# A whole network in one kernel: another order for router, branch, early tiles and the embeddings' product, and other figures for the planner

## The chip, the core and the metric

The kernel runs on one core of a Trainium2 chip. The time is the device time of one execution in microseconds (us). The core has a tensor engine (PE, with a separate weight load, PEld), a vector engine (DVE), a scalar engine (ACT), GpSimd (POOL), and SyncE (SP), whose queue here issues nearly all transfers. Each engine runs its instructions in the order in which they were written, and waits on semaphores for the others.

## What is computed

One block of three parts, then four layers, all in float32 for 256 tokens of width 1024:

```python
h = rms_norm(x, attn_norm_w);  x = x + hybrid_mixer(h, ...)          # SSD and attention
h = rms_norm(x, moe_norm_w);   x = x + hier_moe(h, ...)              # 4 groups x 8 experts
gate = sigmoid(rms_norm(x, ple_norm_w) @ w_ple_gate)
x = rms_norm(x + gate * (p @ w_ple), final_norm_w)                   # embeddings p: 256 x 256
for i in range(4):                          # short conv, neighborhood attention, hyena, short conv
    x = x + mixer_i(rmsnorm(x, norm_mix_g[i]))
    x = x + swiglu(rmsnorm(x, norm_ffn_g[i]), f_w13[i], f_w2[i])
```

In hier_moe a router chooses for each token the best of 4 groups and in it the best 2 of 8 experts:

```python
gl = h @ w_rg + b_rg;  g_oh = one_hot(top1(gl));  g_w = sum(softmax(gl) * g_oh)
el_sel = einsum("blge,blg->ble", el, g_oh);  top_v, top_i = top_k(el_sel, 2)
comb = g_oh * (one_hot(top_i) * softmax(top_v) * g_w)
out = sum over g, e of (silu(h @ w_gate[g, e]) * (h @ w_up[g, e]) * comb[g, e]) @ w_down[g, e]
```

## The kernel before

Tokens lie along the free axis: x is four tiles of 128 x 2 x 256 (x[0] to x[3]). A dense product is made from high and low halves of its operands, three PE instructions of 256 columns each (high by high, high by low, low by high). Its weights come in half tiles of 512 KB (128 x 1024), called raw, in the order of the list `self.order`. ACT copies the high half (wh), DVE subtracts for the low half (wl). There are 7 raw buffers and 5 pairs of wh and wl (`NRAW`, `NSPLIT`).

The experts' weights are 192 such half tiles, used unsplit. A few are loaded ahead of the routing: some into raw buffers, some into the wh and wl buffers (`load_as`), and `NEARLY` of them (early tiles, transfers named raws) into general slots that are not refilled. A buffer of the first two kinds is refilled by `used_up` once its products are issued.

The experts run in eight rounds r, each of four experts: `gate_up(r, 0)`, then `turn(r-1)` and `down(r-1)` (product yo), `gate_up(r, 1)` and `gated(r)`. `moe_back(r)` splits yo into yoh and yol, multiplies with pT (product yb) and adds to x. The routing gives each expert 32 places; a branch (`past()`, L1594) leads to spare code if an expert has more. In this kernel it stands behind round 0. `later()` computes the places of the next three quarters and stands behind it.

The router is in three functions. `route_evac(j)` takes the last sum of x[j], adds it and scales it (xg); `route_pair(j)` multiplies xg for the scores (lg), sums the squares into a column of the same lg, transposes xg (ht) and splits it into hth and htl. `moe()` takes the root rtm of the sums, scales the scores (r_lg) and then walks through some twenty small DVE steps to the choice r_sel; cnt counts places, ph is the selection matrix, and the products hg gather the tokens of the experts from hth and htl.

The tail: `dense(self.each(px), ...)` computes p @ w_ple from the split px with 48 PE instructions, then `ple()` the gate's product from hx (x scaled and split), whose norm comes late: `late_rms` sums squares (ssq), takes a root on ACT (rb), and the evacuation multiplies by it; then a sigmoid on ACT (pg), a product on POOL or DVE, the sum into x, and the next hx.

What sets the order is a planner in the program that builds the kernel. `Clock.cost` gives each instruction a time. Side work (routing, filters of the hyena, attention heads, `moe_back`) is in generators; `pump` puts their next step into PE's stream when the planner's clock says that its inputs are there. `busy(n)` writes products of ones (warm) that keep PE at work while it waits. So other figures in `cost` change places all over the kernel. All instructions have the line L400 of the helper that issues them; they are told apart by names.

Of the kernel before, what the change touches and what calls it, by code (L numbers as in the profile page):

```python
# [21 lines left out]
D = 1024  # L22
# [259 lines left out]
class Clock:  # L282
# [17 lines left out]
    def cost(self, eng, op, out, ins, args, kw):  # L300
        n = self.size(out)
        if "dma" in op:
            return n * out.shape[0] * 4 / 360e3
        if eng == "tensor":
            if op == "transpose":
                return 2 * n / 2400
            x = args[2]
            if x.dtype == F32R:
                return max(n, 256) / 2400 + 0.002
            side = 4 if args[1].shape[-1] == 32 else 1  # L310
            return max(n * (4 if x.dtype == F32 else 1) / side, 64) / 2400 + 0.002
        if eng == "scalar":
# [101 lines left out]
class Net:  # L414
    def __init__(self, ctx, tc, a, taps=None):
# [26 lines left out]
        for r in range(1, 8):  # L442
            self.order += four(r, 0) + four(r - 1, 2) + four(r, 1)
        self.order += four(7, 2) + whole(range(m + 96, nch))
        self.moe_base = m
# [80 lines left out]
    def early(self):  # L526


        while self.nload < self.moe_tiles[0]:
            yield  # L530
        for n in self.early_tiles:
            c, half = self.order[n]
            t = [self.new("raws", shape=(128, 512)) for _ in range(2)]
            self.raw[n], self.kind[n] = t, "slots"
            for i in range(2):
                o = half * 1024 + i * 512
                self.nc.sync.dma_start(t[i], self.a["wst"][c][:, o:o + 512])
            t0 = self.now()
            while self.now() < t0 + EGAP:
                yield  # L540
# [467 lines left out]
    def hybrid(self):  # L1008
# [166 lines left out]
        self.route_begin()  # L1175
        self.side(self.early())
        self.dense(self.each(mx), 8, 4, self.route_evac)
# [241 lines left out]
    def route_evac(self, j, ps):  # L1419

        nc, v = self.nc, self.v
        self.residual(ps, j)
# [10 lines left out]
    def route_pair(self, j, xg, sq):  # L1433
# [15 lines left out]
        h, l = self.new("hth", F32R), self.new("htl", F32R)  # L1449
        yield from self.split_steps(ps, h, l)  # L1450
        self.htok[j] = (h, l)

    def moe(self):
# [12 lines left out]
        self.wait(lambda: htok[3] is not None)  # L1466
        rt = self.sm("rtm", [128, 2, 1])
        self.root(rt, lg_ps[:, :, 36:37], D)
        V.reciprocal(rt, rt)
        rt = rt[:, :, 0]  # L1470
        self.busy(12)

# [98 lines left out]
        self.tap("comb", comb)  # L1571
        next(filt)
        self.sides.append(self.filt)
        rslot, cslot, c4 = m("rslot", 8, 1), m("cslot", 8), m("c4", 8, 4)
        pT = [None] * 4

        def weights(q):
# [9 lines left out]
            V.tensor_reduce(cslot[:, rs], c4[:, rs, :], axis=AX.X, op=ALU.add)  # L1587
            V.tensor_tensor(cslot[:, rs], cslot[:, rs], rslot[:, rs, 0], op=ALU.mult)

        def past():  # L1590
# [74 lines left out]

        px = [None] * 2

        def embeddings():
            pt = self.ld("pt", shape=(128, 2, 256))
            nc.sync.dma_start(pt, self.a["pT"])  # L1670
            yield
            px[:] = yield from self.split_both(pt, "px")

        for r in range(8):
            if r == 7:
                self.side(embeddings())
# [21 lines left out]
        self.hx, self.ssum = [None] * 8, None  # L1698
        self.pp = [None] * 4

        def ple_evac(j, ps):
            self.pp[j] = self.new("pp")
            S.activation(self.pp[j], ps, AF.Copy)

        self.dense(self.each(px), 2, 4, ple_evac)
        self.wait(lambda: self.hx[0] is not None)

    def moe_back(self, r, yo, pT):
# [9 lines left out]
        for j in range(4):  # L1718
# [77 lines left out]
    def ple(self):  # L1796
# [7 lines left out]
        self.fsum = None  # L1804
        norm = self.side(self.late_rms())

# [310 lines left out]
    def filters(self):  # L2117
# [57 lines left out]
        def order(n, cb):  # L2175
            cs = slice(256 * cb, 256 * cb + 256)
            rows = slice(64 * n, 64 * n + 64)
            if n == 0 and cb:
                yield from fetch(cb)
# [6 lines left out]
            F, SD, hl = [], [], []  # L2186
            pss = []
            for t in range(2):
                first = cb == 0 and n == 0
                ps = self.mm_tile("fl") if first else self.sd("fl")  # L2190
# [4 lines left out]
                pss.append(ps)  # L2195
                if first and t == 0:
                    continue
                if first:
                    yield
                for t2, ps in enumerate(pss) if first else ((t, ps),):  # L2200
                    f = self.new("F")
                    V.tensor_tensor(f, ps, dec[t2], op=ALU.mult)
                    F.append(f)
                yield
# [51 lines left out]

        yield from fetch(0)
        load(1)
        while not self.routing:
            yield  # L2260
        first = order(0, 0)
        for _ in range(3):
            next(first)
            yield
# [205 lines left out]
```

## Time and profile before

| | us |
| --- | --- |
| median of 3 runs | 1831.96 (1830.24 to 1832.25) |
| profiled execution, its own time | 1834.63 |
| its span in the profile | 1832.8 |
| PE busy | 1764.5 (96%) |
| DVE busy | 1252.2 (68%) |
| ACT busy | 1019.1 (56%) |
| POOL busy | 514.1 (28%) |
| mean granted clock of PE | 0.986 of full speed |

The span is the time from the first to the last instruction in the trace. Busy time says which engine was at work, not which one was waited for; a wait is read from what stood idle and what ended it. The network goes through in this order: the hybrid mixer to 317 us, router and experts to 563, the gate with the embeddings to 606, then the four layers.

### The profile page before, as it was taken

The numbers are of one execution on the slowest core, as the hardware profiler recorded it, in microseconds if no ns is written. First come the engines' busy times: TensorE is split into PE (matmuls) and PEld (weight loads), VectorE is DVE, ScalarE is ACT, GpSimd is POOL, SyncE is SP. The second block draws the span as 40 slices with busy tenths as digits, with TensorE's granted clock in tenths as the row PEclk, the third lists the DMA queues.
The fourth block names the chain that finished last, engine by engine and source line by source line (L and its number), as shares of the span: only waits on it lengthen the run. The fifth ranks groups of instructions, "written<-read, shape, count | busy, mean of one in ns | idle before, by whom it ended". The sixth has DMA issues, their size and how long they took to land. (4 is left out here: it accounts for less than half of the span.)

```text
span 1832.8 us, 30301 instructions
## 1 busy us (share of the span) xinstructions
PE 1764.5 (96%) x11603; PEld 1491.7 (81%) x11603; DVE 1252.2 (68%) x1758; ACT 1019.1 (56%) x1754; POOL 514.1 (28%) x532
## 2 busy tenths in 40 slices
PE   9999999888888899999999999999899999999998
PEld 8897899453236899888987888899898888888887
DVE  6677655322125987886687788668978876888873
ACT  7787644332225656554566655566556555666552
POOL 3635440242440341220122122017611210501210
PEclk9999999998999999999999999999999999999999
DMA  8443359799998575555544455565435555656552
GB/s 284 145 147 116 116 171 337 274 402 406 409 406 292 166 246 180 188 187 181 184 150 147 146 185 186 174 206 174 150 118 193 189 181 182 190 163 210 184 191 74
DMA packets 114909, 377.14 MB, mean 206 GB/s; under 512 B 12449, under 2 KB 22057, under 8 KB 114761
## 3 DMA queue, kind: packets, MB, share of 16 engines
q1 hardware_dynamic: 114568, 375.03, 60.1%
q8 instruction: 92, 1.51, 0.3%
q14 instruction: 57, 0.46, 0.1%
q0 software_dynamic: 48, 0.13, 0.0%
q10 hardware_dynamic: 144, 0.00, 0.0%
HBM read 369.87 MB, written 5.25 MB: 205 GB/s over the span
## 5 line engine op out<-in xcount | busy, mean ns | idle before, releaser
L400 PE MATMUL mm<-hx,wh 128*128 128x256 f32 (+1 forms) x3712 | 936.1, 331 | 7.3 <-ACT hx L400 5.1
L400 DVE TENSOR_TENSOR wl<-raw,wh 128x1024 fp32r<-128x1024 f32 (+1 forms) x486 | 681.2, 1411 | 214.9 <-ACT wh L400 192.5
L400 PE MATMUL mm<-hx,wl 128*128 128x256 f32 x2576 | 727.6, 282 | 0.6 <-DVE wl L400 0.6
L400 PEld LDWEIGHTS mm<-hx,wh 128*128 128x128 f32 x3712 | 628.4, 191 | 86.8 <-issue 8.5
L400 ACT ACTIVATE wh<-raw 128x1024 fp32r<-128x1024 f32 (+1 forms) x486 | 507.9, 1053 | 294.6 <-PE mm L400 133.6
L400 PEld LDWEIGHTS mm<-hx,wl 128*128 128x128 f32 x2576 | 491.0, 191 | 1.2 <-DVE wl L400 1.2
L400 PE MATMUL mm<-fx,wh 128*128 128x512 f32 x704 | 248.9, 399 | 0.0
L400 POOL TENSOR_TENSOR t<-mo,rb 128x512 f32<-128x512 f32 x80 | 103.5, 1293 | 406.1 <-DVE mo L400 393.0
L400 PE MATMUL mm<-fx,wl 128*128 128x256 f32 x704 | 197.7, 281 | 0.0
L400 PEld LDWEIGHTS mm<-fx,wh 128*128 128x128 f32 x704 | 132.3, 188 | 33.0
L400 PEld LDWEIGHTS mm<-fx,wl 128*128 128x128 f32 x704 | 133.0, 189 | 0.0
L400 POOL TENSOR_TENSOR acc<-acc,sq 128x512 f32<-128x512 f32 x20 | 33.5, 1677 | 315.9 <-ACT sq L400 315.8
L400 DVE TENSOR_TENSOR mo<-mo,mm 128x256 f32<-128x256 f32 x220 | 82.5, 416 | 21.3 <-ACT mo L400 21.3
L400 ACT ACTIVATE fx<-t 128x256 fp32r<-128x256 f32 x88 | 36.5, 416 | 104.6 <-DVE t L400 104.6
L400 ACT ACTIVATE mo<-mm 128x256 f32<-128x256 f32 x220 | 73.7, 375 | 35.9 <-PE mm L400 35.1
L400 PE MATMUL gu<-raw,hg 128*32 128x512 f32 x468 | 78.7, 624 | 3.7 <-DMA raw<-in_wst 3.7
L400 PE MATMUL mm<-yx,wh 128*128 128x256 f32 (+1 forms) x320 | 69.8, 308 | 0.0
L400 DVE TENSOR_TENSOR fx<-t,fx 128x256 fp32r<-128x256 f32 x88 | 37.3, 425 | 37.7 <-ACT fx L400 37.7
L400 ACT ACTIVATE hx<-x,vec 128x256 fp32r<-128x256 f32 x72 | 32.8, 502 | 53.1 <-DVE x L400 51.2
L400 PEld LDWEIGHTS mm<-yx,wh 128*128 128x128 f32 x320 | 51.8, 191 | 4.3 <-issue 1.3
L400 PE MATMUL mm<-yx,wl 128*128 128x256 f32 x192 | 54.2, 282 | 0.0
L400 PEld LDWEIGHTS gu<-raw,hg 128*32 128x32 f32 x468 | 15.9, 112 | 45.6 <-DMA raw<-in_wst 22.0
(389 smaller groups left out, 2443.3 us busy)
## 6 DMA issues: line engine op xcount, KB each, us to landing
raw<-in_wst SPq DMA_DIRECT2D x663, 512.0 KB, 4.7
raws<-in_wst SPq DMA_DIRECT2D x22, 256.0 KB, 7.4
hs<-H SPq DMA_DIRECT2D x16, 256.0 KB, 5.2
Hl<-hs SPq DMA_DIRECT2D x16, 256.0 KB, 11.3
tb<-in_rpbt SPq DMA_DIRECT2D x16, 192.0 KB, 4.8
dec<-in_decay SPq DMA_DIRECT2D x8, 256.0 KB, 7.1
x<-in_xT SPq DMA_DIRECT2D x4, 256.0 KB, 5.1
raw<-in_wst SPq DMA_DIRECT2D x4, 256.0 KB
```

The costliest lines, as they stand in the source:

```text
L400: return f(*args, **kw)
```

## The change

It rewrites five places.

1. The planner's figures: a product costs 0.0135 us beside its columns where it cost 0.002, and a transfer goes at 400 GB/s where it went at 360. The distance between filter steps (FGAP) is 18 instead of 20, the number of early tiles (NEARLY) 13 instead of 11, and their distance (EGAP) 1.3 instead of 1.5. The early tiles begin behind those in raw, wh and wl buffers, and `moe()` issues the rest of them at its start.
2. The router: for the last tile, x is added in halves, the root is taken ahead of the transposes, and htl is made by ACT (htf) and POOL instead of DVE. One DVE step of the choice is gone. The first filter's products, which stood ahead of lg, come later.
3. The branch stands behind round 1, `later()` ahead of `gate_up(1, 1)`.
4. The embeddings' product is side work from round 6 on, with its own transfers (wp, four of 256 KB), splits (wph, wpl) and products (pp, four groups of 12).
5. The gate: the table of the root is loaded in `moe_back` of round 7, that of the sigmoid right after the root; two of four products are on DVE.

```diff
-NRAW, NSPLIT, NSLOT, NLOAD, WARM, LAG, FGAP, BMOST, PARK = 7, 5, 46, 6, 11, 4.0, 20, 12, 14
-NEARLY, EGAP = 11, 1.5
+NRAW, NSPLIT, NSLOT, NLOAD, WARM, LAG, FGAP, BMOST, PARK = 7, 5, 46, 6, 11, 4.0, 18, 12, 14
+NEARLY, EGAP = 13, 1.3
...
-            return n * out.shape[0] * 4 / 360e3
+            return n * out.shape[0] * 4 / 400e3
...
-                return max(n, 256) / 2400 + 0.002
+                return max(n, 256) / 2400 + 0.0135
...
-        self.early_tiles = range(2 * m + NRAW, 2 * m + NRAW + NEARLY)
+        first = 2 * m + NRAW + 2 * NSPLIT
+        self.early_tiles = range(first, first + NEARLY)
...
-            t0 = self.now()
-            while self.now() < t0 + EGAP:
+            t0, self.clock.mark = self.now(), 0.0
+            while self.now() < t0 + EGAP and not self.routing:
...
+        if j < 3:
+            self.residual(ps, j)
         for o in range(2):
+            if j == 3:
+                nc.vector.tensor_tensor(self.x[j][:, o, :], self.x[j][:, o, :], ps[:, o, :], op=ALU.add)
             nc.scalar.activation(xg[:, o, :], self.x[j][:, o, :], AF.Copy, scale=v("moe", 2 * j + o))
...
+        if j == 3:
+            self.rtok = self.sm("rtm", [128, 2, 1])
+            self.root(self.rtok, self.lg_ps[:, :, 36:37], D)
+            nc.vector.reciprocal(self.rtok, self.rtok)
         ps = self.sd("ht", reads=2)
...
-        yield from self.split_steps(ps, h, l)
+        if j == 3:
+            f = self.new("htf")
+            nc.scalar.activation(h, ps, AF.Copy)
+            nc.scalar.activation(f, ps, AF.Copy)
+            nc.gpsimd.tensor_tensor(l, f, h.bitcast(F32), op=ALU.subtract)
+        else:
+            yield from self.split_steps(ps, h, l)
...
-        filt = self.filt[0]
-        next(filt)
-        next(filt)
+        self.busy(6)
+        while self.ahead in self.sides:
+            self.step(self.ahead)
...
-        tt(oh2, oh2, bc(tm8), op=ALU.is_equal)
-        tt(oh2, oh2, bc(goh), op=ALU.mult)
+        tt(oh2, rev8, bc(tm8), op=ALU.is_equal)
...
+            for j in range(4):
+                w = self.new("wp", shape=(128, 512))
+                nc.sync.dma_start(w, self.a["wst"][self.moe_base + 96][:, 512 * j:512 * j + 512])
...
+                for k in range(2):
+                    for o in range(2):
+                        i = slice(128 * (2 * k + o), 128 * (2 * k + o) + 128)
+                        self.three(ps[:, o, :], h[:, i], l[:, i], px[k], k == 0 and o == 0, k == 1)
...
         for r in range(8):
-            if r == 7:
+            if r == 6:
                 self.side(embeddings())
...
+            if r == 1:
+                self.side(later())
             gate_up(r, 1, ps)
+            self.wait(lambda: r // 2 in weighed)
             gated(r, ps)
-            if r == 0:
+            if r == 1:
                 past()
-                self.side(later())
                 self.routed = True
...
-        self.dense(self.each(px), 2, 4, ple_evac)
...
+                if j == 0:
+                    nc.scalar.activation(self.sm("warm4", [128, 1]), self.eps, AF.Sqrt)
...
+        def scale():
+            yield from self.late_rms()
+            S.activation(self.sm("warm5", [128, 1]), self.eps, AF.Sigmoid)
...
-            eng = V if j == 3 else G
+            eng = V if j in (0, 3) else G
...
-        yield from self.flow([first] + [order(n, cb) for cb in range(4) for n in range(2)][1:], FGAP, 2)
+        yield from self.flow([order(n, cb) for cb in range(4) for n in range(2)], FGAP, 3)
```

SP's queue from the last early tiles to the branch, before (raws are early tiles, raw those in buffers, `mosti` the number that the branch looks at):

```order
L400 DMA raw<-in_wst 128x1024
L400 DMA raws<-in_wst 128x512 x2
L400 DMA raw<-in_wst 128x1024 x11
L400 DMA raws<-in_wst 128x512 x2
L400 DMA raw<-in_wst 128x1024 x7
L1592 TENSOR_LOAD mosti
L1592 ISA x2
L1594 COMPARE_AND_BRANCH
```

The same place of the changed kernel:

```order
L400 DMA raw<-in_wst 128x1024
L400 DMA raws<-in_wst 128x512 x4
L400 DMA raw<-in_wst 128x1024 x39
L1602 TENSOR_LOAD mosti
L1602 ISA x2
L1604 COMPARE_AND_BRANCH
```

Before, the last two halves of an early tile stood behind eleven other tiles, and seven tiles stood between them and the branch; now all early tiles stand ahead, and 39 tiles stand between them and the branch.

ACT in the tail, from the splits ahead of the root rb to the sigmoids pg, before:

```order
L400 ACTIVATE sq<-x_98 128x512
L400 ACTIVATE wh<-raw 128x1024 x2
L400 ACT_TABLE_LOAD
L400 ACTIVATE rb<-ssq,eps 128x256
L400 ACTIVATE wh<-raw 128x1024 x2
L400 ACT_TABLE_LOAD
L400 ACTIVATE pg<-pg 128x512 x3
```

The same place of the changed kernel:

```order
L400 ACTIVATE sq<-x_98 128x512
L400 ACTIVATE pp<-pp 128x512
L400 ACTIVATE wh<-raw 128x1024
L400 ACTIVATE rb<-ssq,eps 128x256
L400 ACT_TABLE_LOAD
L400 ACTIVATE warm_6340<-eps 128x1
L400 ACTIVATE wh<-raw 128x1024 x2
L400 ACTIVATE pg<-pg 128x512 x3
```

The load ahead of rb has gone to an earlier place, and the one ahead of pg stands right behind rb, ahead of two splits.

PE in the neighborhood attention, between the first head's sums qkn and its transposes qkt, as a difference:

```order
 L400 MATMUL mm<-hx,wh 128x256 x2
 L400 MATMUL mm<-hx,wl 128x256
-L400 MATMUL mm<-hx,wh 128x256 x2
-L400 MATMUL mm<-hx,wl 128x256
-L400 MATMUL mm<-hx,wh 128x256 x2
-L400 MATMUL mm<-hx,wl 128x256
-L400 MATMUL mm<-hx,wh 128x256 x2
-L400 MATMUL mm<-hx,wl 128x256
 L400 MATMUL qkt<-cst,sqq 128x128 x2
```

Nine products of the dense stream that stood ahead of qkt stand behind it now; for the four groups of heads the distances were 18, 19, 34 and 32 products and are 9, 6, 23 and 28.

## Rows read from the trace of the kernel before

**Rows 1.** busy by stretch: us; PE, PEld, DVE, ACT, POOL; clock; DMA share; GB/s
```profile
0.00:317.00 317.00, 308.45 (x2333) 281.58 (x2334) 206.56 (x343) 213.79 (x377) 131.85 (x141) 0.99 0.56 185
317.00:563.30 246.30, 211.85 (x1352) 99.81 (x1350) 60.53 (x140) 62.61 (x128) 88.43 (x104) 0.94 0.97 380
563.30:606.50 43.20, 35.28 (x259) 34.23 (x259) 33.03 (x38) 29.34 (x41) 8.04 (x5) 0.92 0.71 241
606.50:1832.80 1226.30, 1208.95 (x7662) 1076.06 (x7662) 952.06 (x1239) 713.38 (x1209) 285.81 (x283) 1.00 0.54 175
```

**Rows 2.** the same view, the experts' stretch at and behind the branch
```profile
345.00:357.00 12.00, 12.00 (x90) 4.88 (x83) 0.00 (x0) 2.69 (x5) 1.48 (x2) 0.90 0.70 234
357.00:561.00 204.00, 175.94 (x1082) 78.82 (x1080) 48.95 (x90) 52.20 (x109) 80.64 (x96) 0.95 1.03 406
```

**Rows 3.** timeline of SP's queue: start, us until the last issue, engine, line, transfer
```profile
318.29 1.56 SPq L400 DMA_DIRECT2D raws<-in_wst  x2
333.97 18.14 SPq L400 DMA_DIRECT2D raw<-in_wst  x13
```

**Rows 4.** waits of SP, and instructions of the branch, 327 to 352
```profile
SPq L1594 <- SPq L1594: 8.5, 4, 5.0
...
L1594 PEldq COMPARE_BRANCH  x1: 6252/6252/6252, 338.1 to 338.1; - x1
```

**Rows 5.** timelines of PE, ACT and DVE in the router
```profile
320.17 1.09 PE L400 MATMUL ht<-cst,xg 128*128 128x128 f32 x4
...
321.79 0.26 ACT L400 ACTIVATE rtm<-lg,eps 128x2 f32<-128x2 f32 x1
...
321.93 0.69 DVE L400 TENSOR_TENSOR htl<-ht,hth 128x512 fp32r<-128x512 f32 x1 [3.74 <-ACT hth L400]
322.53 0.16 DVE L400 RECIPROCAL rtm<-rtm 128x2 f32<-128x2 f32 x1
322.72 0.42 DVE L400 SCALAR_TENSOR_TENSOR r_lg<-lg,rtm,vec 128x36 f32<-128x36 f32 x2
...
326.15 0.22 DVE L400 TENSOR_TENSOR r_oh<-r_oh,r_goh 128x64 f32<-128x64 f32 x1
```

**Rows 6.** DMA issues 357 to 560: KB each, median us from issue to landing
```profile
raw<-in_wst SPq DMA_DIRECT2D x148, 512.0 KB, 9.6
```

**Rows 7.** timeline of PE in the tail, [idle before <-releaser]
```profile
561.39 1.90 PE L400 MATMUL yo<-raw,hTs 128*32 128x512 f32 x10 [0.21 <-DMA raw<-in_wst]
565.06 0.50 PE L400 MATMUL mm<-px,wh 128*128 128x256 f32 x2 [1.76 <-ACT wh L400]
...
573.18 0.28 PE L400 MATMUL yb<-pT,yoh 128*128 128x256 f32 x1
573.30 0.28 PE L400 MATMUL yb<-pT,yol 128*128 128x256 f32 x1
...
575.14 0.90 PE L400 MATMUL mm<-hx,wh 128*128 128x256 f32 x2 [1.32 <-ACT hx L400]
...
594.14 0.59 PE L400 MATMUL ssq<-ssum,ones 128*128 128x256 f32 x2
...
606.44 0.38 PE L400 MATMUL mm<-hx,wh 128*128 128x256 f32 x1 [3.81 <-ACT hx L400]
607.31 0.58 PE L400 MATMUL mm<-hx,wh 128*128 128x256 f32 x1 [0.48 <-DVE hx L400]
```

**Rows 8.** timeline of ACT behind ssq
```profile
594.62 1.28 ACT L400 ACT_TABLE_LOAD   x1
595.92 0.48 ACT L400 ACTIVATE rb<-ssq,eps 128x256 f32<-128x256 f32 x1
```

**Rows 9.** busy table again, the start of the next layer
```profile
606.70:610.10 3.40, 2.92 (x14) 2.79 (x14) 2.83 (x5) 2.60 (x7) 0.28 (x1) 0.50 0.28 92
```

**Rows 10.** waits of PE behind 606.6, the largest and the smallest (us, times, longest)
```profile
PE ci L400 <- DVE l L400: 4.6, 3, 2.2
...
PE U L400 <- DVE cm L400: 0.2, 1, 0.2
```

More of the change, by code (lines that the diff above doesn't have):

```diff
@@ L308, in cost @@
             if x.dtype == F32R:
-                return max(n, 256) / 2400 + 0.002
+                return max(n, 256) / 2400 + 0.0135
             side = 4 if args[1].shape[-1] == 32 else 1
-            return max(n * (4 if x.dtype == F32 else 1) / side, 64) / 2400 + 0.002
+            return max(n * (4 if x.dtype == F32 else 1) / side, 64) / 2400 + 0.0135
         if eng == "scalar":
@@ L443, in __init__ @@
             self.order += four(r, 0) + four(r - 1, 2) + four(r, 1)
-        self.order += four(7, 2) + whole(range(m + 96, nch))
+        self.order += four(7, 2) + whole(range(m + 97, nch))
         self.moe_base = m
@@ L1175, in hybrid @@
         self.route_begin()
-        self.side(self.early())
+        self.ahead = self.side(self.early())
         self.dense(self.each(mx), 8, 4, self.route_evac)
@@ L1421, in route_evac @@
         nc, v = self.nc, self.v
-        self.residual(ps, j)
         xg = self.xg[j] = self.new("xg")
+        if j < 3:
+            self.residual(ps, j)
         for o in range(2):
+            if j == 3:
+                nc.vector.tensor_tensor(self.x[j][:, o, :], self.x[j][:, o, :], ps[:, o, :], op=ALU.add)
             nc.scalar.activation(xg[:, o, :], self.x[j][:, o, :], AF.Copy, scale=v("moe", 2 * j + o))
@@ L1466, in moe @@
         self.wait(lambda: htok[3] is not None)
[L1467 to L1471, printed above, removed]
+        rt = self.rtok[:, :, 0]
+        self.busy(10)
         m = lambda name, *shape: self.sm("r_" + name, [128, *shape])
@@ L1571, in moe @@
         self.tap("comb", comb)
-        next(filt)
         self.sides.append(self.filt)
         rslot, cslot, c4 = m("rslot", 8, 1), m("cslot", 8), m("c4", 8, 4)
-        pT = [None] * 4
+        pT, weighed = [None] * 4, []
         def weights(q):
@@ L1588, in weights @@
             V.tensor_tensor(cslot[:, rs], cslot[:, rs], rslot[:, rs, 0], op=ALU.mult)
+            weighed.append(q)
         def past():
@@ L1664, in down @@
             back.append(self.side(self.moe_back(r, yo, pT), *yo))
-        px = [None] * 2
+        self.pp = [None] * 4
         def embeddings():
@@ L1671, in embeddings @@
             yield
-            px[:] = yield from self.split_both(pt, "px")
+            px = yield from self.split_both(pt, "px")
+            for j in range(4):
+                w = self.new("wp", shape=(128, 512))
+                nc.sync.dma_start(w, self.a["wst"][self.moe_base + 96][:, 512 * j:512 * j + 512])
+                yield
+                h, l = self.new("wph", F32R, (128, 512)), self.new("wpl", F32R, (128, 512))
+                yield from self.split_steps(w, h, l)
+                yield
+                ps = self.sd("pp")
+                for k in range(2):
+                    for o in range(2):
+                        i = slice(128 * (2 * k + o), 128 * (2 * k + o) + 128)
+                        self.three(ps[:, o, :], h[:, i], l[:, i], px[k], k == 0 and o == 0, k == 1)
+                yield
+                p = self.new("pp")
+                S.activation(p, ps, AF.Copy)
+                self.pp[j] = p
+                yield
         for r in range(8):
-            if r == 7:
+            if r == 6:
                 self.side(embeddings())
@@ L1698, in moe @@
         self.hx, self.ssum = [None] * 8, None
[L1699 to L1703, printed above, removed]
-        self.dense(self.each(px), 2, 4, ple_evac)
         self.wait(lambda: self.hx[0] is not None)
@@ L1804, in ple @@
         self.fsum = None
-        norm = self.side(self.late_rms())
+        def scale():
+            yield from self.late_rms()
+            S.activation(self.sm("warm5", [128, 1]), self.eps, AF.Sigmoid)
+        norm = self.side(scale())
         def evac(j, ps):
@@ L1814, in gate @@
             yield
-            eng = V if j == 3 else G
+            while self.pp[j] is None:
+                yield
+            eng = V if j in (0, 3) else G
             eng.tensor_tensor(t, t, self.pp[j], op=ALU.mult)
@@ L2177, in order @@
             rows = slice(64 * n, 64 * n + 64)
-            if n == 0 and cb:
+            if n == 0:
                 yield from fetch(cb)
@@ L2186, in order @@
             F, SD, hl = [], [], []
-            pss = []
             for t in range(2):
-                first = cb == 0 and n == 0
-                ps = self.mm_tile("fl") if first else self.sd("fl")
+                ps = self.sd("fl")
                 for di in range(2):
@@ L2194, in order @@
                         nc.tensor.matmul(ps[:, di, :], x[rows, o:o + 128], w[rows, di, :], start=(i == 0), stop=(i == 2))
[L2195 to L2203, printed above, removed]
+                f = self.new("F")
+                V.tensor_tensor(f, ps, dec[t], op=ALU.mult)
+                F.append(f)
                 yield
@@ L2255, in order @@
             yield
-        yield from fetch(0)
+        load(0)
         load(1)
[L2259 to L2264, printed above, removed]
         while not self.routed:
             yield
-        yield from self.flow([first] + [order(n, cb) for cb in range(4) for n in range(2)][1:], FGAP, 2)
+        yield from self.flow([order(n, cb) for cb in range(4) for n in range(2)], FGAP, 3)
     def hyena(self, i):
```

## The prediction

> **What bounds the kernel now.** I read the busy table by stretch first: it divides the span at the places where the bound changes [rows 1]. Before 317 us PE is busy 308.45 of 317.00 us, and after 606.5 us it is busy 1208.95 of 1226.30: there the kernel runs at PE's speed, and only a wait of PE can be won. The experts' stretch, 317 to 563.3, is another case: PE 211.85 of 246.30, but the DMA share is 0.97. In the 43.20 us between it and the next layer PE has 35.28, DVE 33.03 and ACT 29.34: chains, no single bound.
>
> Inside the experts' stretch the second view is the table of DMA rates [rows 2]. From 357 to 561 the engines move 406 GB/s at a share of 1.03: full, so this part ends when the bytes have passed. Two places are not. The SP timeline [rows 3] shows the first: after the last early half tiles (318.29) nothing is issued until 333.97, when the first used buffer is refilled. The second is 345:357 with 234 GB/s [rows 2], and the waits [rows 4] say why: the branch (L1594) holds SP for 8.5 us, and PE's sequencer for 6252 ns.
>
> So: in the experts' stretch count DMA time not used; in the tail follow the chain; elsewhere look at waits of PE.
>
> **Part 1, router and early tiles.** A 512-KB tile takes 524288 B / 406 GB/s = 1.29 us. Two more of them (NEARLY 11 to 13) are in place before the first refill, in time in which the engines now rest; each shortens the full part by one tile: -2.6. Bounds: 0 if the slots come free too late to load them in the gap, -2.6 otherwise; I take the whole, as the gap of some 14 us [rows 3] has room for two tiles.
>
> The router's chain starts the refills. Now the root rtm stands on ACT behind hth and starts at 321.79, its reciprocal on DVE behind htl (321.93), and r_lg starts at 322.72 [rows 5]. The moved root needs only the sums in lg, done when PE goes on to ht (320.17): its 0.26 and the 0.16 of the reciprocal, with the distances between engines, give r_lg at about 320.8, -1.9. The residual of the last x in halves lets xg begin some 0.3 earlier (half of a 128x512 operation on DVE, 0.69 as htl), and of the DVE steps one of 0.22 goes (r_oh, 326.15) [rows 5]. Sum -2.4. The 12 filter products that leave the place ahead of lg lie under the wait for xg and cost nothing either way; they go to a stretch where PE rests 34 us. htl on POOL may come 1 us later than on DVE, but the gathers that read it come only after the whole routing.
>
> **Part 2, the branch.** In 345:357 the engines move (1 - 234/406) of 12.00 us too little: -5.1 us if the hole vanished [rows 2]. The change puts the branch one round later. Now SP reaches it with seven refills issued, the first tiles after a pause. Later, in the steady part, a tile lands 9.6 us after its issue at the median [rows 6]: that much work is queued when SP stops for 8.5 us. Then the engines need not run dry, though SP must catch up; I leave 1.3 of the 5.1: -3.8. Bounds 0 and -5.1. The pieces that later() places now run ahead of the branch; DVE and ACT have three quarters of that stretch free.
>
> The Trainium skill speaks against this part (page "Runtime: NRT & Kernel Launch", section Instruction fetch mechanics): a taken branch whose target is not in the fetched window forces a fetch before work goes on. The trace agrees in so far as the sequencers stop for 8.5 and 6.3 us; the page gives no price, and by it alone the stop would be moved and nothing won, which is rival 1.
>
> **Part 3, the queue's end.** Two of the four 256-KB pieces of w_ple and one 256-KB store stand on SP ahead of the last expert tile, where nothing of the kind stood: 3 x 0.65 = +1.9 on a full queue. The other tiles behind the last expert tile come as much earlier as one 512-KB piece leaves the queue; nobody waits for them.
>
> The last expert product therefore ends 2.4 + 2.6 + 3.8 - 1.9 = 6.9 us earlier.
>
> **Part 4, the tail.** From the end of the last yo (561.39 + 1.90 = 563.29) to the first product of the gate (575.14) it is 11.85 us [rows 7]. In it stands the embeddings' product px (565.06 to 573.18), ahead of the yb products that the gate waits for. Now half of it (24 of 48 products) stands in the experts' stretch, where PE rests. Left over is the chain yo, split, yb, x, hx: the part from yb to the gate is 575.14 - 573.18 = 1.96, and I put some 3.6 for the two splits of yo with their distances, 5.5 in all: -6.3. The other 24 products, among the gate's, cost 24 x 0.12 = +2.9 (yb at 573.18 and 573.30 [rows 7]). On the far side ssq (594.14) to the first product of the next layer (606.44) is a chain of 12.3 us: with a table load of 1.28 ahead of rb [rows 8] and another ahead of the sigmoids pg. Both loads leave it, placed earlier on ACT where nothing waits for it: 2.6 us shorter; and about seven more groups of three products of the gate now stand behind ssq, 2.5 us more cover. The waits of 3.81 and 0.48 [rows 7] go: -4.3. That sums to -7.7. But DVE is busy 33.03 of 43.20 [rows 1], and in a tail of 35.5 us it would have no rest at all; I leave 1.2 for that: -6.5. Bounds: -3 if DVE sets the tail, -7.7 if nothing does. After that last wait PE stands at clock 0.50 for 3.4 us (606.7:610.1, busy 2.92) [rows 9]; without the wait there is no rest before it: -1.7, or 0.
>
> The Trainium skill would give more here (page "ScalarE: Activation LUTs", section What ACT_TABLE_LOAD costs): a load of 1283 ns and a drain of about 1380 ns, 2.66 us a switch. The trace shows the 1.28 and rb 0.02 us behind it, no drain; by the page two loads off the chain would be 5.3 instead of 2.6, and as the wait of PE that they feed is gone by either, the sum is the same.
>
> **Part 5, the planner's figures.** They are no instruction, but they reorder all of the kernel. The trace gives 0.12 from one 256-column product to the next [rows 7]: the old figure (0.1087) lets the planner run 10% ahead of the chip, the new one (0.1202) fits. With the old figure a side step is put 10% more products behind its input than planned, which acts as padding. The order shows it in the neighborhood attention: between qkn and qkt there were 18, 19, 34 and 32 products, now 9, 6, 23 and 28. PE's waits outside the stretch 317 to 606.5 are 14 rows, from 4.6 to 0.2, 19.5 us in all, of which side chains have 13.3 [rows 10]. Steps nearer to their inputs start sooner but wait more if anything is late. Bounds: -13 (no such wait is left) and +15 (rival 4). With the same work on all engines I take a little of the cost, +3.
>
> **Sum.** -6.9 - 6.5 - 1.7 + 3 = -12.1. The profiled run took 1834.63 us (its span 1832.8), 2.7 above the median of the three runs, 1831.96; the difference is laid on the median: 1819.9, say 1820, and with the bounds of the parts 1814 to 1826.
>
> **Rivals.**
> 1. The hole at the branch moves with the branch. For it: SP and PE are stopped as long as before [rows 4], and SP refills nothing for 8.5 us while PE frees buffers. Against it: the 9.6 us in the queue [rows 6]. It gives back 3.8: 1824.
> 2. The tail is set by DVE and ACT: of 43.20 us DVE has 33.03 busy [rows 1], and splits of w_ple take the place of those of the old product, and the waits move from hx to wl. Gives back 3.5 and the 1.7 of the clock: 1825.
> 3. No difference: rivals 1 and 2 together, or half of part 5's upper bound on top of one of them: about 1830.
> 4. Slower: the lost padding. It needs chains that come as late as the old planner's 10% covered: in the four places counted above 37 products fewer are cover that is lost, 37 x 0.12 = 4.4 us, if each place has none to spare. The attention heads of the first stretch and the hyena's ci and U steps are built in the same way; if all three lose as much with some clock behind it, PE waits 15 to 20 us more. Against it: ahead of each, other work can be chosen, and ACT and DVE have 42% and 22% of the late stretch free [rows 1]. It decides from 12 us on, and gives 1832 - 15 + 22 = 1839.
> 5. More is won: side steps that start sooner shrink the 13.3 us instead: about 1809.
>
> **How the numbers follow.** Forecast 0.45; rival 1 0.12; rival 2 0.12; rival 3 0.14; rival 4 0.12; rival 5 0.05. A measurement of this kernel tells about 0.2%, 3.7 us, from no change, so forecast and rivals 1, 2 and 5 are faster (0.74), rival 3 is the same (0.14), rival 4 slower (0.12). The range takes in the forecast and rivals 1 to 3 and leaves out 4 and half of 5: 1810 to 1834, of which the forecast's own is 1814 to 1826.
>
> **What would show it.** Part 1: the first refill 2 to 3 us earlier after the last product of the mixer, and a gap on SP of some 11 us. Part 2: SP still stopped for about 8.5 us at the branch, but no stretch under 350 GB/s behind it; if a stretch of 12 us stands near 234 again, rival 1. Part 3: wp and one store among the last refills. Part 4: less than 6.5 us from the last yo to the first product of the gate, no wait of hx above 1 us at the next layer and no half clock there; waits on wl or x instead speak for rival 2. Part 5: the sum of PE's waits outside the two middle stretches near 19.5; above 30, rival 4. I am wrong if PE's waits ahead of 317 or behind 606.5 grow by more than the middle wins.

## The result and the profile after the change

The changed kernel takes 1854.11 us (median of 4 runs, 1851.07 to 1855.17) beside 1832.11 us of the kernel before: ratio 1.0115 (95% interval 1.0100 to 1.0129). It is slower by 21 us by the ratio (22.0 by the medians), outside the range given. Rival 4 had the sign and the mechanism, but put it at 1839.

The busy table of the changed kernel, cut at the same four landmarks as [rows 1] (end of the mixer's last product, end of the last yo, first product of the next layer, end; columns as there):

```profile
0.00:335.93 335.93, 318.33 (x2333) 288.58 (x2334) 211.02 (x341) 211.12 (x374) 131.80 (x141) 0.95 0.52 175
335.93:580.49 244.56, 213.67 (x1386) 108.23 (x1384) 68.25 (x143) 67.06 (x135) 89.50 (x105) 0.94 0.98 385
580.49:618.22 37.73, 32.04 (x236) 30.98 (x235) 32.41 (x38) 25.95 (x39) 7.40 (x4) 0.91 0.72 248
618.22:1849.30 1231.08, 1208.06 (x7630) 1075.32 (x7630) 947.63 (x1242) 716.48 (x1214) 289.10 (x284) 1.00 0.54 174
```

With the kernel before cut at the same landmarks (316.73, 563.29, 606.44) the four parts moved by +19.2 (335.93 against 316.73), -2.0 (244.56 against 246.56), -5.4 (37.73 against 43.15) and +4.7 us (1231.08 against 1226.36). The sum is the difference of the spans, 1849.3 - 1832.8 = 16.5. The medians differ by 22.0: the profiled run of the kernel before (1834.63) lies above its median, and that of the changed kernel (1851.07) is the fastest of its four, so the profiles leave some 5 us without a place. The parts that the change rewrites became shorter, as forecast though by less, and the loss is in the mixer and in the layers, where the change has few lines of its own (transfers of the early tiles and of the filters, the distance FGAP). The planner's figures reach all of it; e1 and e3 below try them apart from the rest.

In the mixer PE does the same 2333 instructions, at a mean clock of 0.95 instead of 0.99. The places are in PE's timeline (start, us, tile, count, [idle before <-releaser]):

```profile
70.73 0.69 PE L400 MATMUL xtok<-cst,cu 128*128 128x128 f32 x2 [2.54 <-ACT cu L400]
...
104.31 1.65 PE L400 MATMUL s<-t,t 64*128 64x128 f32 x4 [1.89 <-DVE ast L400]
...
131.17 0.87 PE L400 MATMUL pt<-cst,P 128*128 128x128 f32 x3 [1.48 <-ACT PT L400]
...
161.17 0.52 PE L400 MATMUL pt<-cst,P 128*128 128x128 f32 x3 [1.10 <-ACT PT L400]
```

and behind each of these waits the busy table shows the granted clock (third column from the end) at about half:

```profile
70.70:77.00 6.30, 6.27 (x32) 6.27 (x33) 4.10 (x7) 6.05 (x12) 3.76 (x6) 0.54 0.22 75
104.30:113.50 9.20, 8.45 (x25) 5.57 (x26) 4.91 (x19) 2.07 (x9) 0.00 (x0) 0.50 0.35 114
131.20:134.80 3.60, 3.60 (x18) 3.47 (x20) 3.60 (x1) 0.70 (x2) 3.60 (x5) 0.54 0.00 0
161.20:169.00 7.80, 7.80 (x44) 5.23 (x46) 3.64 (x9) 3.74 (x14) 2.37 (x3) 0.56 0.19 69
```

A 2.54-us wait ahead of xtok is followed by 6.3 us at 0.54, and the 1.89 ahead of s by 9.2 us at 0.50 (with a second wait of 0.74 in it, at 109.21). What such a wait costs here is the wait and half of the slow stretch behind it (not every wait has one, see e2 below).

The hyena (1221.0 to 1367.4 before, both waits of [rows 10] lie there) shows the rest, as the same view of both kernels shows. Before:

```profile
1221.00:1367.40 146.40, 136.87 (x1047) 130.66 (x1047) 125.45 (x158) 91.27 (x160) 80.06 (x74) 0.98 0.45 148
```

After:

```profile
1231.40:1382.80 151.40, 136.38 (x1042) 130.69 (x1041) 123.87 (x157) 92.32 (x160) 79.51 (x74) 0.98 0.44 143
```

It is 5.0 us longer with the same work, and PE rests 15.0 us in it instead of 9.5. From the next layer's first product to the hyena, with the neighborhood attention in it, nothing was lost. Before and after:

```profile
606.44:1221.00 614.56, 611.96 (x3939) 542.93 (x3940) 477.31 (x644) 363.30 (x618) 122.81 (x125) 1.00 0.56 180
618.22:1231.40 613.18, 610.60 (x3920) 542.03 (x3921) 477.16 (x646) 364.17 (x621) 126.09 (x125) 1.00 0.56 181
```

The branch's hole has moved with the branch. The same two views as [rows 2] and [rows 4], of the changed kernel:

```profile
390.00:402.00 12.00, 11.53 (x95) 6.18 (x98) 1.84 (x6) 4.15 (x9) 5.34 (x6) 0.98 0.69 232
...
SPq L1604 <- SPq L1604: 8.8, 4, 5.0
```

The next two are SP's last issue ahead of the branch and its first behind it:

```profile
383.09 0.41 SPq L400 DMA_DIRECT2D raw<-in_wst  x1
...
393.59 0.35 SPq L400 DMA_DIRECT2D raw<-in_wst  x1
```

12 us at 232 GB/s are (1 - 232/406) x 12 = 5.1 us lost, the very price of before (5.1 at 234).

In the tail the product of the gate starts 3.55 us after the last yo (584.04 - 580.49), where it was 11.85 [rows 7], but the waits are not all gone:

```profile
584.04 0.90 PE L400 MATMUL mm<-hx,wh 128*128 128x256 f32 x2 [2.36 <-ACT hx L400]
...
586.18 0.58 PE L400 MATMUL mm<-hx,wl 128*128 128x256 f32 x1 [1.23 <-DVE wl L400]
...
618.22 0.91 PE L400 MATMUL mm<-hx,wh 128*128 128x256 f32 x2 [1.71 <-ACT hx L400]
```

### The profile page after: what moved, and what is told of

It reads as the page before. It is cut to its first block, busy times and chain, and to the rows that moved or that the text cites. A ratio compares the mean times of both kernels' runs of the same rounds, so it can differ in the third digit from the quotient of the medians.

```text
span 1849.3 us, 30299 instructions
## 1 busy us (share of the span) xinstructions
PE 1772.1 (96%) x11579; PEld 1503.1 (81%) x11579; DVE 1259.3 (68%) x1762; ACT 1020.6 (55%) x1761; POOL 517.8 (28%) x534
## 3 DMA queue, kind: packets, MB, share of 16 engines
HBM read 369.87 MB, written 5.25 MB: 203 GB/s over the span
## 4 chain that ended last, share of the span: by engine, by line
PE 64%; DMA 7%; POOL 3%; DVE 2%; issue 1%; ACT 1%; SPq 0%; DVEq 0%; POOLq 0%; ACTq 0%
PE mm L400 56%; DMA raw<-in_wst 6%; PE gu L400 1%; PE s L400 1%; POOL cx L400 1%; PE hg L400 1%; PE mmr L400 1%; DMA Hl<-hn 1%; PE ci L400 1%; DVE wl L400 1%; POOL cm L400 1%; PE yb L400 1%; POOL eo L400 1%; PE fl L400 0%; DMA dec<-in_decay 0%
```

## Experiments

All were measured beside the kernel before on the same chip. The tables below use the landmarks: mixer (start to the end of its last product), experts (to the end of the last yo), tail (to the next layer's first product), rest.

**The planner's figures, one at a time.** e1 takes back the product's figure alone:

```diff
-                return max(n, 256) / 2400 + 0.0135
+                return max(n, 256) / 2400 + 0.002
...
-            return max(n * (4 if x.dtype == F32 else 1) / side, 64) / 2400 + 0.0135
+            return max(n * (4 if x.dtype == F32 else 1) / side, 64) / 2400 + 0.002
```

> The changed kernel with the planner's old figure for a product (0.002 us beside its columns), all else as changed. Theory A, the product's figure: with the true duration the planner puts a side step right behind its input, PE waits where the input is late, and the clock falls to half behind it; the changed mixer is 19 us longer for that alone. Then the mixer ends near 317 us again and the time is 1824 to 1830. Theory B, the rework itself (later transfers of the filters, more early tiles, two more filters in flight) crowds DVE, ACT and POOL in the mixer: then the mixer still ends near 336 us and the time is 1848 to 1855.

1829.49 us, ratio 0.9987 (0.9977 to 0.9997). The mixer ends at 317.77. Theory A holds: one number in a cost function is worth 23 us by the two ratios, and without it the change is a small gain.

e2 takes back the transfers' figure alone:

```diff
-            return n * out.shape[0] * 4 / 400e3
+            return n * out.shape[0] * 4 / 360e3
```

> The changed kernel with the planner's old figure for transfers (360 GB/s), the product's figure as changed. Theory A: no difference to the changed kernel, 1850 to 1857, mixer end near 336 us. Rival: the transfers' figure makes the planner split weights too early in the mixer; then the mixer ends 5 us or more earlier and the time is below 1847.

1844.62 us, ratio 1.0067 (1.0050 to 1.0084), mixer end 323.38. My expectation failed and the rival's numbers held (that weights are split too early, its reason, was not looked at): the transfers' figure is worth some 9 us beside the new product figure; the mixer is 12.5 us shorter, and some is lost again in the experts (247.32). Beside the old product figure it does no such thing (e1 has 400 GB/s).

e3 is the kernel before with both new figures and nothing else:

```diff
-            return n * out.shape[0] * 4 / 360e3
+            return n * out.shape[0] * 4 / 400e3
...
-                return max(n, 256) / 2400 + 0.002
+                return max(n, 256) / 2400 + 0.0135
...
-            return max(n * (4 if x.dtype == F32 else 1) / side, 64) / 2400 + 0.002
+            return max(n * (4 if x.dtype == F32 else 1) / side, 64) / 2400 + 0.0135
```

> The kernel before with both new figures of the planner and nothing else of the change. Theory A: slower than before by the 19 us of the mixer and the 5 us of the hyena, 1850 to 1860, with half-clock stretches between 60 and 170 us. Theory B: 1830 to 1836, clock full in the mixer.

1861.01 us, ratio 1.0163 (1.0138 to 1.0188), just above the 1850 to 1860 expected. The figures alone cost 30 us by the ratio; router, branch, early tiles and embeddings take about 9 back (1.0115 for the whole change). Its clock falls in the same region, 60 to 170 us:

```profile
60.00:170.00 110.00, 98.58 (x654) 81.79 (x656) 65.83 (x121) 75.22 (x153) 45.33 (x47) 0.86 0.30 98
```

where e1, with the new code and the old product figure, has

```profile
60.00:170.00 110.00, 106.30 (x811) 90.28 (x813) 75.45 (x159) 81.88 (x182) 57.50 (x56) 0.98 0.34 111
```

e4 keeps the true figure and gives slack by name, as a longer distance between engines:

```diff
-LINK, SELF, REFILL = 0.15, 0.12, 1.22
+LINK, SELF, REFILL = 0.30, 0.12, 1.22
```

> The changed kernel with the planner's distance between engines (LINK) at 0.30 us instead of 0.15, the product's figure as changed: slack is given by name instead of by a wrong duration. Theory A: most of the mixer's 19 us come back, 1828 to 1842. Theory B, or a theory by which it is the choice of which side work goes first and not the slack: 1846 or more.

1836.79 us, ratio 1.0023 (1.0013 to 1.0033), mixer end 323.32: 17 of the 21 us come back while the figure stays, as theory A said. So slack given by another name does most of what the small figure did. That it does so by the slack alone, and not by the other order that comes with it, is not shown.

e7 goes the other way, more slack than before:

```diff
-                return max(n, 256) / 2400 + 0.0135
+                return max(n, 256) / 2400 - 0.008
...
-            return max(n * (4 if x.dtype == F32 else 1) / side, 64) / 2400 + 0.0135
+            return max(n * (4 if x.dtype == F32 else 1) / side, 64) / 2400 - 0.008
```

> The changed kernel with the planner's figure for a product 0.008 us below its columns (0.099 us for 256, against 0.109 in the kernel before and 0.120 as changed). Theory A: slack is what helps, and a little more of it helps the mixer no further once its waits are gone: mixer end 314 to 320 us, time 1826 to 1836. Rival: the old figure is the optimum and each step away costs; then side work comes late, the mixer or the hyena loses 5 us or more, 1835 or above.

1830.06 us, ratio 0.9991 (0.9981 to 1.0000), inside theory A's range; but the mixer was better than expected, 311.47, shorter than in the kernel before by 5 us, and the experts (247.06) and the rest (1232.59) took it back.

Seven profiles now have the same work in the mixer and different orders. "Waits" is the sum of PE's waits there, "slow clock" the sum of (1 - granted clock) over its stretches of 2 us:

| kernel | product, transfer figure | mixer us | waits | slow clock | what is left |
| --- | --- | --- | --- | --- | --- |
| e7 | -0.008, 400 | 311.5 | 6.2 | 3.4 | 301.9 |
| before | 0.002, 360 | 316.7 | 8.4 | 3.4 | 304.9 |
| e1 | 0.002, 400 | 317.8 | 10.0 | 3.4 | 304.4 |
| e4 | 0.0135, 400, LINK 0.30 | 323.3 | 12.0 | 6.8 | 304.5 |
| e2 | 0.0135, 360 | 323.4 | 15.4 | 1.7 | 306.3 |
| changed | 0.0135, 400 | 335.9 | 17.5 | 15.4 | 303.1 |
| e3 (old code) | 0.0135, 400 | 339.6 | 19.2 | 17.1 | 303.3 |

What is left is within 302 to 306 us in all of them, while the mixer goes from 311 to 340. So the large differences are waits and clock; one of a few us is not explained so (e7 is 5.2 us shorter than the kernel before, and 3.0 of them are in what is left). It also tells what happened in e2: nearly the waits of the changed kernel (15.4 against 17.5), but hardly a slow stretch behind them. A wait of 1.57 us, which ends at 92.17, is as long as those of the changed kernel and has full clock behind it:

```profile
92.20:102.20 10.00, 9.38 (x76) 7.79 (x76) 6.48 (x8) 9.83 (x20) 3.70 (x3) 1.00 0.36 120
```

Which waits are followed by half clock and which are not, the seven profiles don't settle.

**The branch.** The changed kernel's SP stops for 8.8 us. e5 is e1 with the transfers of the spare code (never run with these inputs) on POOL's queue:

```diff
-                nc.sync.dma_start(w, src(k // 4, (k % 4) * 512))
+                nc.gpsimd.dma_start(w, src(k // 4, (k % 4) * 512))
...
-                    nc.sync.dma_start(w[f], src(2, f * 1024 + n * 512))
+                    nc.gpsimd.dma_start(w[f], src(2, f * 1024 + n * 512))
```

> As e1 (the changed kernel with the old product figure), and the transfers in the spare code behind the branch are issued by POOL instead of SP; that code is not run with these inputs. Theory A: the hole in the DMA rate behind the branch (233 GB/s over 12 us, 5 us lost) is SP's own price for skipping a piece of code with its transfers, 8 to 9 us; with none of its transfers there SP is back sooner, the hole shrinks to 0 to 2 us and the time falls by 3 to 5 us to about 1825. Theory B: SP pays for the branch itself (fetch of the target) whatever it skips; then the hole stays near 5 us and the time is 1828 to 1832.

1825.69 us, ratio 0.9970 (0.9958 to 0.9983): 3 us less than e1 by the ratios, whose intervals just overlap; experts 240.82 instead of 244.32. The hole is nearly closed, 375 GB/s over the 12 us where e1 has 233:

```profile
368.00:380.00 12.00, 12.00 (x106) 6.93 (x98) 2.31 (x5) 5.12 (x10) 9.00 (x10) 1.00 1.01 375
...
361.80 1.61 SPq L400 DMA_DIRECT2D raw<-in_wst  x2
...
369.06 0.35 SPq L400 DMA_DIRECT2D raw<-in_wst  x1
```

SP's last tile ahead of the branch is issued at 361.80 + 1.61 = 363.4 and the next at 369.06, 5.6 us instead of 10.1 in e1 (364.48 + 0.33 to 374.95). What went are eight semaphore instructions that SP worked through behind the branch, as the view of the branch's line in e1 shows them (durations in ns, then the first and last start):

```profile
L1604 SPq EVENT_SEMAPHORE  x8: 17/17/17, 370.8 to 374.8; - x8
```

What stays is the load of the number and the branch itself. In e5's stop the DMA view (364 to 369.1 us) has two packets of instructions, 0.02 MB in all. That fits a fetch of the target, though the view does not say for which engine they are. Theory A holds for 4.5 of the 10 us, theory B for the rest, which the queued transfers cover.

e12 is the same edit in the kernel before:

> The kernel before with the transfers of the spare code behind the branch issued by POOL instead of SP (the code is not run with these inputs), and nothing of the change. Theory A: the place of the branch never mattered, and what SP pays for skipping its transfers does: the hole behind the branch (5.1 us lost in 345:357) shrinks here as it did from e1 to e5, and the time falls by 3 to 5 us to 1827 to 1829. Theory B: behind round 0 nothing is queued when SP stops, and PE's own 4.5 us at the branch keep the hole open: 1830 to 1833.

1833.33 us, ratio 1.0007 (0.9997 to 1.0016): no gain, theory B. Behind round 0 the hole is as before, but now made by PE:

```profile
SPq L400 <- PE gu L400: 26.3, 5, 14.0
...
PE gu L400 <- PEq L1594: 4.3, 1, 4.3
...
345.00:357.00 12.00, 12.00 (x90) 5.36 (x82) 0.00 (x0) 2.70 (x5) 1.28 (x1) 0.88 0.72 237
```

SP's own wait at the branch is gone, yet it waits for gu products to free buffers (26.3 us, of which 14.0 lie ahead of the first refill), PE waits 4.3 us at the branch, and 345:357 stays at 237 GB/s. So each half alone is worth nothing: at the later place PE's stop is covered (in e1 it lasts 6.0 us, and 354:361 has 404 GB/s), the edit of e5 shortens SP's, and only both close the hole.

**What stands ahead of the experts.** e6 is e1 with the first filter transfers after the routing:

```diff
-        load(0)
-        load(1)
         while not self.routed:
             yield
+        load(0)
+        load(1)
```

> As e1, and the first transfers of the filters (load(0), load(1)) are issued after the routing instead of before the early tiles, so that SP does not stop for a free buffer (dec waits 6.9 us for dftl in e1) ahead of the experts' tiles. Theory A: bytes that did not pass in that wait are what keeps the experts' stretch from being shorter; with the wait gone it ends 2 to 4 us sooner, 1825 to 1828. Theory B: the engines were waiting for buffers anyway there; no difference, 1828 to 1832.

1834.95 us, ratio 1.0015 (1.0005 to 1.0024): 5 us slower than e1, which neither theory said. SP's early tiles do start 8 us sooner (279.5 instead of 287.2), but then SP stands until the first buffer is free (the wait lies within the first row):

```profile
304.05 41.18 SPq L400 DMA_DIRECT2D raw<-in_wst  x25
...
SPq L400 <- PE gu L400: 17.4, 4, 16.2
```

16.2 us against 9.2 in e1: the time won ahead of the routing became a longer hole, and the filters' six pieces of 256 KB (3.9 us at 406 GB/s) now pass behind it. The experts' stretch is 7.7 us longer (251.98 against 244.32); what makes the other half of that is open. In these runs only what is removed from behind the first refill shortens the experts' stretch.

e11 is e5 with 11 early tiles:

```diff
-NEARLY, EGAP = 13, 1.3
+NEARLY, EGAP = 11, 1.3
```

> As e5 with 11 early tiles as before the change instead of 13. Theory: two tiles more then have to pass in the full part behind the first refill, 2 x 1.29 = 2.6 us: experts' stretch 243.4 instead of 240.8, 1827 to 1829. Rival: the tiles passed at the cost of others and the two are worth nothing: 1825 to 1826.

1829.12 us, ratio 0.9984 (0.9973 to 0.9994), beside 0.9970 of e5: 2.6 us slower by the ratios, as expected, but the intervals overlap; in the profile the experts are 4.5 us longer. That the two tiles are worth something is likely, that it is 2.6 us is not shown.

e9 is e5 with products of ones in PE's wait for the choice:

```diff
-        self.busy(10)
+        self.busy(22)
```

> As e5 (old product figure, spare code without SP's transfers), and 22 instead of 10 products of ones ahead of cnt in the router. In e1 and e5 PE waits 2.65 us for r_sel there and the gathers hg behind it run at half clock. Theory A: that wait is what gave back the router's gain; filled, hg takes 4.0 us instead of 5.25 to the first expert product, and the experts' stretch ends 1.0 to 1.5 us sooner, 1824 to 1825. Rival: the products delay cnt, or the stretch is bound elsewhere: no difference, 1825 to 1827.

The wait is filled and the clock is full: from hg to the first expert product it takes 4.00 us instead of 5.25. The time is 1824.70, ratio 0.9964 (0.9951 to 0.9976), beside 0.9970 (0.9958 to 0.9983) of e5; the difference is not clear of the noise, and the experts' stretch is not shorter (241.39). Half of theory A: the router's gain was lost there, but getting it back is worth 1 us by the ratios, which cannot be told from nothing.

**The tail.** e8 is e1 without the two activations that load tables early:

```diff
-                if j == 0:
-                    nc.scalar.activation(self.sm("warm4", [128, 1]), self.eps, AF.Sqrt)
...
-            S.activation(self.sm("warm5", [128, 1]), self.eps, AF.Sigmoid)
```

> As e1 without the two activations that load the tables of the root and of the sigmoid ahead of time. Theory: the two loads of 1.28 us go back onto the chain from ssq to the next layer's first product, where 1.7 us of wait are left in e1: 2.0 to 3.5 us longer from the last expert product to the next layer (37.0 in e1), 1830 to 1834. Rival: one load is hidden behind splits of weights anyway: 1.3 us or less.

1827.88 us, ratio 0.9983 (0.9974 to 0.9993), beside 1829.49 of e1; the tail is 36.39 instead of 37.00. My theory fell and the rival held: taking table loads off the chain is worth nothing here (from ssq to the next layer 12.00 us instead of 11.63). What the tail gains must come from the rest of the edit, the embeddings' product above all; the product moved to DVE was not tried alone.

**Two figures.** e10 is e5 with the product figure of e7 in the mixer and that of the kernel before after it:

```diff
-                return max(n, 256) / 2400 + 0.002
+                return max(n, 256) / 2400 + self.product
...
+        self.product = -0.008
...
         self.routing = True
+        self.clock.product = 0.002
```

> As e5, with the product figure 0.008 us below the columns until the routing and 0.002 above them after it. Theory A: the mixer wants more slack (311.5 in e7, 316.2 in e5) and the rest less of it (1232.6 in e7, 1228.9 in e5); so the mixer ends near 311.5, the other parts as in e5: 1818 to 1823. Rival: the parts hang together (what is loaded when the mixer ends), and the experts' stretch gets as long as in e7 (247 instead of 241): 1823 to 1829.

1824.89 us, ratio 0.9959 (0.9949 to 0.9970), no better than e9. The mixer is 314.63, but the experts 246.62, near the 247 of e7: as the rival said, the parts hang together. That this goes by what has been loaded when the mixer ends was not counted. e5, e9 and e10 are all faster than both kernels, by 5 to 8 us against the one before, and cannot be told apart.

## Why the prediction was wrong

| term | forecast | measured |
| --- | --- | --- |
| experts' stretch: router, tiles, branch, queue's end | -6.9 | -2.0 |
| tail, with its half clock | -6.5 - 1.7 | -5.4 |
| planner's figures, elsewhere | +3 | +19.2 + 4.7 |
| sum, on the spans | -12.1 | +16.5 |

**Part 5 is the step that failed**, by 21 us: +3 was forecast for the planner's figures, and the mixer and the rest took 23.9. Rival 4 (chance 0.12) had named the mechanism and, with 22 us, nearly the size; it came to 1839 only because it took off 15 us for the other parts, of which 7.4 came. The price in part 5 was wrong in two ways. Lost cover was counted in four places of the neighborhood attention, where the order showed it and where nothing was lost (613.18 us instead of 614.56), and not in the mixer, where the chains of SSD and attention run side by side, nor in the hyena; rival 4 names both without a count. And I priced a wait by its length. In the changed mixer waits grew by 9.1 us (17.5 - 8.4) and slow clock by 12.0 (15.4 - 3.4): the larger half, which rival 4 had only as "some clock behind it", though I had priced that very effect in the tail [rows 9]. The argument "the new figure fits the chip" was the trap: the too small figure had been giving slack ahead of side work, and e4 shows that slack of another name restores most of it. Which of the planner's other figures are too small, so that the slack is needed, was not tried, and stays open.

**Part 2.** Rival 1 came out word for word: the hole is the same. Against it I had set 9.6 us from issue to landing. But after SP's last issue (383.09 + 0.41 = 383.5) the rate holds for some 7 us only, 406 GB/s to 390 and then:

```profile
390.00:391.00 1.00, 1.00 (x8) 1.00 (x8) 0.69 (x1) 0.00 (x0) 1.00 (x2) 0.76 0.73 283
391.00:392.00 1.00, 1.00 (x11) 0.36 (x13) 0.00 (x0) 0.60 (x1) 0.92 (x2) 1.00 0.32 123
```

SP's next issue is at 393.59: its stop lasts 10.1 us, not 8.5, since the load of the number and the way back count too. The time from issue to landing is not the time that a queue lasts. The Trainium skill (page "Runtime: NRT & Kernel Launch", section Instruction fetch mechanics), by which a taken branch out of the fetched window stops an engine, spoke for rival 1. The trace agrees for about half of the stop: 5.6 us stay in e5 with none of its transfers left to skip, and two packets of instructions pass in them.

**Part 1.** The two tiles are not contradicted (e11: 2.6 us by the ratios, as forecast, but not clear of the noise). The router did get shorter, but by less: from the mixer's end to cnt it is 8.40 us (344.33 - 335.93) where it was 9.96, -1.6 instead of -2.4, and then the gain is lost in the next step:

```profile
344.33 0.20 PE L400 MATMUL cnt<-r_sel,trib 128*128 128x64 bf16 x1 [2.65 <-DVE r_sel L400]
...
345.00:350.00 5.00, 4.85 (x29) 4.69 (x28) 2.29 (x13) 2.29 (x4) 0.00 (x0) 0.66 0.60 238
```

cnt came sooner, PE's wait for it got longer (2.65 instead of 1.67), and the gathers behind ran at half clock. From the mixer's end to the first expert product it is 15.28 us, before 15.30. PE was through with what stands ahead of cnt 5.75 us after the mixer's end (339.28 + 2.40 - 335.93) instead of 8.29 (321.05 + 3.97 - 316.73), 2.5 us sooner, and cnt came only 1.6 sooner. The filter products are not the reason: twelve products of ones stand in their place (1.50 us at 335.77), and that they cost nothing either way holds as far as the trace shows. What I left out is that the kernel before has a slow stretch of the same length here:

```profile
320.00:323.40 3.40, 3.40 (x18) 3.40 (x18) 1.41 (x6) 2.04 (x3) 0.00 (x0) 0.50 1.02 410
```

There it lies on the transposes and on the products of ones ahead of the wait (24 in 3.97 us, where the changed kernel has 20 in 2.40), and for the products of ones nobody waits. In the changed kernel these run at full clock, the wait is longer, and the slow stretch lies on the gathers, which the experts wait for. In e9, with the wait filled, the gathers run at full clock.

**Part 3** cannot be told from part 1: -2.0 would be -2.6 (tiles) + 1.9 (queue's end), both as forecast, and a remainder of -1.3.

**Part 4** was right in size for the start: 11.85 to 3.55 is -8.3 (forecast -6.3). The far side was wrong. From ssq (605.08) to the next layer's first product (618.22) it is 13.1 us, before 12.3: the table loads left the chain, and in this order DVE took their place, much as rival 2 said:

```profile
613.00 1.79 DVE L400 TENSOR_TENSOR pg<-pg,pp 128x512 f32<-128x512 f32 x1
614.71 2.31 DVE L400 TENSOR_TENSOR wl<-raw,wh 128x1024 fp32r<-128x1024 f32 x1
616.94 0.68 DVE L400 TENSOR_TENSOR x<-x,pg 128x512 f32<-128x512 f32 x1
```

The product moved from POOL to DVE takes 1.79 us there, beside POOL's own two products (612.89 to 615.94); the other one on DVE takes 0.68. A split of weights of 2.31 stands behind it and ahead of the x that the next layer waits for. In e1, the same code in another order, the product takes 0.68 us and the chain 11.63. The wait fell from 3.81 + 0.48 to 1.71, by the longer cover and not by a shorter chain. The -1.7 did not come at all: behind the wait the clock is at half for as long as in [rows 9].

```profile
619.20:622.60 3.40, 3.40 (x18) 3.40 (x17) 2.14 (x5) 3.40 (x9) 1.32 (x1) 0.50 0.49 172
```

The Trainium skill's price for a table switch (page "ScalarE: Activation LUTs", section What ACT_TABLE_LOAD costs, 2.66 us with a drain) again finds no drain in the trace: the early load takes 1.28 us, and the next activation on ACT starts at its end:

```profile
582.10 1.28 ACT L400 ACT_TABLE_LOAD   x1
583.39 0.20 ACT L400 ACTIVATE warm<-eps 128x1 f32<-128x1 f32 x1
```

## What to carry to other kernels

A planner that orders instructions by estimated times has errors that balance each other: correcting one to its measured value can remove slack that others needed, and the loss shows up far from the edit. Price a wait of the tensor engine by the wait and by the slow stretch that may follow it. Where transfers set the end, count only bytes and idle time behind the first refill, and hold a stop of the issuing queue against how long its queued transfers last after the last issue.

## What the runs showed of the hardware

Waits of PE of 1.1 to 2.5 us in the mixer were followed by 3.6 to 9.2 us at about half clock, and 9.1 us of added waits came with 12.0 us of slow clock; in e2 waits of 15.4 us came with 1.7. A taken branch costs SP more where the skipped code holds its transfers: eight semaphore instructions took 4.0 us (370.8 to 374.8), on top of some 5 us that SP pays in any case; PE's branch took 6.0 to 6.3 us in the kernel before, e1, e5 and e12, but 0.36 us in the changed kernel (358 ns) and 0.35 in e4 and e6, and why is open. An operation of DVE that takes 0.68 us took 1.74 to 1.79 where POOL computed at the same time (the product at 613.00 in the changed kernel, the sum into x at 604.11 in the kernel before). Two kernels whose branch stands in different places answered differently to the same edit (e5 and e12), so neither a place nor a price can be judged alone.
